# Low halves of split weights formed by an adding transfer, with five vector-engine priorities and a regrouped up-projection

## The chip, the core and the metric

The kernel runs on one core of one Trainium2 chip. The metric is the device time of one execution in microseconds (us). The core has a tensor engine (PE, with weight loads listed apart as PEld), a vector engine (DVE), a scalar engine (ACT), GpSimd (POOL), the sync engine (SP), which here only issues transfers, and 16 DMA engines, which all queues share. Each engine runs its own instructions in a fixed order and waits at the head of that order for semaphores.

## What is computed

A trunk of two layers over 1024 tokens of width 1024. Each layer normalises its input, projects it with one wide matrix, runs four head groups on parts of the projection (A: matrix memory, B: RWKV-7 with a delta rule, C: a gated linear recurrence, D: retention), gates each with its own SiLU path, and maps the four results back with one output projection, which is normalised and added to the input. Cut to what matters here:

```python
for l in range(DEPTH):                        # 2
    h = rms_norm(x, norm_pre[l])
    p = h @ w_in[l]                           # 1024 x 1024 @ 1024 x 7824
    ...
    decay_logit = rwkv_w0[l] + jnp.tanh(w_lo) @ rwkv_w_up[l]
    a_b = jax.nn.sigmoid(rwkv_a0[l] + a_lo @ rwkv_a_up[l])
    ...
    y = jnp.concatenate([y_a, y_b, y_c, y_d], axis=-1) @ w_out[l]   # 2048 -> 1024
    x = x + rms_norm(y, norm_post[l])
```

## The kernel before, in words

Large products are done in the fp32r type, with three products in place of one: every operand is split into a rounded part (hi) and what is left (lo), and hi x hi, hi x lo and lo x hi are added in PSUM. Activations are split once per layer (`hT`). Weights are split as they are loaded, by `load_piece` (line 365): a transfer on SP brings 128 x 512 values into a tile `raw` (2 buffers), ACT rounds them into `hi` (4 buffers), and DVE subtracts `hi` from `raw` into `lo` (4 buffers). A program on one layer loads 186 such tiles, 372 in all: 180 for channel pieces (`wch`), 64 for token pieces (`wa`, `wd`) and 128 for the output projection (`wo`).

A layer has two stages. In the **mixing stage**, pieces of the input projection and the steps of the head groups share PE. A channel piece (`ch_piece_of`, line 412) uses 2 weight tiles, a token piece (`tok_piece_of`, line 452) uses 4, which are all the buffers there are. `Driver` (line 489) writes the order of the program: it keeps a planner's clock (`Clock`, line 147, with guessed durations for every operation), lets a head group take its next step when the planner says that its inputs are ready, and puts six matmuls of a piece wherever no group is ready; a piece is loaded one piece ahead. Every instruction goes through the recording wrapper on line 255, so nearly all rows of the profile carry that line and are told apart by their tiles. After that the tile framework's own list scheduler sets the final order on each engine; code under `tc.high_priority()` is preferred there among instructions that it holds to be ready.

The head groups carry states from chunk to chunk. Group B (`unit_b`, line 773) keeps `bS`: a matmul `psbc<-bS,TQ` (line 1025), then two DVE instructions, one for each head, write the next `bS` (line 1028). Group A (`unit_a`) keeps `aS` (line 1187) and group D (`unit_d`) keeps `dS` (line 1292), each also with two DVE instructions a chunk. `prep` in group B (line 808) starts with the two up-projections: for each of two outputs a matmul with all 128 rows (`luh`) and one with 64 rows (`lul`); their operand `lora` is brought by 32 transfers issued from POOL (line 822), the only transfers there. POOL also computes the power -0.5 of each normalisation (`rsq`, line 362; 128 of them), which DVE waits for.

In the **output stage** (`out_product`, line 1358) two halves of 512 tokens each run over 16 steps. A step has 24 matmuls of 512 columns, and for the step ahead loads two weight tiles and two activations (`ymix`, `zmix`), 256 KB each. While the second half runs, the first half is normalised and stored (`finish`, line 1398), with further transfers and DVE work.

Of the kernel before, what the change touches and what calls it, by code (L numbers as in the profile page):

```python
# [17 lines left out]
F32 = mybir.dt.float32  # L18
F32R = mybir.dt.float32r
AF = mybir.ActivationFunctionType  # L20
ALU = mybir.AluOpType
# [240 lines left out]
def trunk(ctx: ExitStack, tc, x, wch, wa, wd, wg, wo, pv, gb, lup, lrw, npost, cst, dtab, out):  # L262
# [102 lines left out]
    def load_piece(src, n=512):  # L365

        raw = T("raw", (128, 512))
        lo = T("lo", (128, 512), F32R)
        hi = T("hi", (128, 512), F32R)
        DQ.dma_start(raw[:, :n], src)  # L370
        A.copy(hi[:, :n], raw[:, :n])
        V.tensor_tensor(lo[:, :n], raw[:, :n], hi[:, :n].bitcast(F32), ALU.subtract)
        return hi[:, :n], lo[:, :n]
# [399 lines left out]
    def unit_b(l, P, hTs, j, drv):  # L773
# [34 lines left out]
        def prep(qt):  # L808
# [22 lines left out]
            for n, p in enumerate((wps, aps)):  # L831
                hp = slice(64 * n, 64 * n + 64)
                PE.matmul(p[:, 0:QB], lu[0][:, n, :], lo_[:, n, :], start=True, stop=False)
                PE.matmul(p[:, 0:QB], lu[1][hp], lo_[hp, n, :], start=False, stop=True)
# [108 lines left out]
        def mix(qt):  # L943
# [65 lines left out]
            for e in range(2):  # L1009
                p3 = pss[e][:, 0:CP * 128].rearrange("p (c t) -> p c t", c=CP)  # L1010
                V.tensor_tensor(TQ[:, e::2, 0:64], AR[:, :, 2 + e, :], p3[:, :, 0:64], ALU.subtract)
                V.tensor_tensor(TQ[:, e::2, 64:128], id64.unsqueeze(1).to_broadcast((128, CP, 64)), p3[:, :, 64:128], ALU.subtract)
# [8 lines left out]
            for c in range(CB):  # L1021
# [4 lines left out]
                for h in range(2):  # L1026
                    hp = slice(64 * h, 64 * h + 64)
                    V.tensor_scalar(bS[(n + 1) % 2][hp, hp], yc[64:128, hp], wc[64:128, h, c:c + 1], None, ALU.mult)
# [60 lines left out]
    def unit_a(l, P, hTs, j, drv):  # L1089
# [28 lines left out]
        def mix():  # L1118
# [3 lines left out]
            for qt in range(S // QA):  # L1122
# [35 lines left out]
                for h in range(2):  # L1158
                    D = Ds[h]
                    V.scalar_tensor_tensor(D, pss[h][:, 0:QA], 1.0 / 32, D, ALU.mult, ALU.mult)  # L1160
                    pk.append(D)
# [7 lines left out]
                for c in range(NQ):  # L1169
# [12 lines left out]
                    for h in range(2):  # L1182
                        hp = slice(64 * h, 64 * h + 64)
                        if st is None:
                            V.tensor_copy(st2[hp, 65 * h:65 * h + 65], o[hp, 256 + 65 * h:256 + 65 * h + 65])
                            continue
                        V.scalar_tensor_tensor(st2[hp, 65 * h:65 * h + 65], st[hp, 65 * h:65 * h + 65], sc[hp, c:c + 1],
                                               o[hp, 256 + 65 * h:256 + 65 * h + 65], ALU.mult, ALU.add)
# [23 lines left out]
    def unit_d(l, P, hTs, j, drv):  # L1212
# [28 lines left out]
        def mix():  # L1241
# [5 lines left out]
            for qt in range(4):  # L1247
# [29 lines left out]
                for c in range(2):  # L1277
# [9 lines left out]
                    for h in range(2):  # L1287
# [4 lines left out]
                        V.scalar_tensor_tensor(st2[hp, hp], st[hp, hp], G128[2 * j + h], o[hp, so + 64 * h:so + 64 * h + 64], ALU.mult, ALU.add)  # L1292
# [285 lines left out]
```

## Time and profile before

| What | Value |
|---|---|
| Median of 3 runs | 2529.39 us (2527.3 to 2534.37) |
| The profiled execution's own time | 2524.98 us |
| Span of its instructions | 2523.1 us, mean granted TensorE clock 0.992 |
| Instructions | 45012, of them 32064 matmuls and weight loads |
| Bytes by DMA | 265.82 MB, mean 105 GB/s |

PE's busy time is from modelled ends, so that a busy PE may still be a waiting one; its waits are read from the weight loads (PEld), which stand at the head of the same queue. A wait row names the engine and the tile that waits, what it waited for, and the total in us, how often, and the longest.

### The profile page before, as it was taken

Reading aid. Unit: us, or ns where it says so; the run is one execution under the profiler, and the core shown is the slowest. Engines: PE = TensorE matmul, PEld = TensorE weight load, DVE = VectorE, ACT = ScalarE, POOL = GpSimd, SP = SyncE. Lnnn points to the kernel's source line nnn. Section 1 sums busy time; section 2 is a strip of 40 time slices with the busy share of each in tenths; the row PEclk is TensorE's granted clock in tenths of the full one; section 3 lists DMA queues with packets and bytes.
Section 4 is the critical chain, followed back from the end, with each engine's and each line's share of the span. In section 5 each row is a group of like instructions: output and inputs, shape, how many; then the busy total and the mean of one; then the engine's idle time right before and its main releaser. Section 6 shows DMA issues by size and latency. Waiting matters only on the chain.

```text
span 2523.1 us, 45012 instructions
## 1 busy us (share of the span) xinstructions
PE 2383.7 (94%) x16032; PEld 1955.2 (77%) x16032; DVE 1794.0 (71%) x5724; ACT 1054.0 (42%) x2325; POOL 193.7 (8%) x306
## 2 busy tenths in 40 slices
PE   7999999999999999999999999999999999999998
PEld 5797887787787777887677878877877877788876
DVE  6678878878778875435577787888788778744464
ACT  5334433543543553323354344335445435522233
POOL 1201100010000000000012001000000000000000
PEclk9999999999999999999999999999999999999999
DMA  5323233232222233655633232332323222326564
GB/s 160 101 72 88 62 78 99 67 84 71 91 76 75 75 88 103 194 162 176 196 119 103 68 93 74 78 90 68 81 72 90 69 79 76 102 94 217 172 198 153
DMA packets 219237, 265.82 MB, mean 105 GB/s; under 512 B 72708, under 2 KB 122244, under 8 KB 219012
## 3 DMA queue, kind: packets, MB, share of 16 engines
q1 hardware_dynamic: 210308, 254.54, 33.9%
q0 software_dynamic: 8704, 8.39, 1.4%
q8 instruction: 127, 2.08, 0.3%
q14 instruction: 98, 0.80, 0.1%
HBM read 201.76 MB, written 61.08 MB: 104 GB/s over the span
## 4 chain that ended last, share of the span: by engine, by line
PE 47%; DVE 28%; DMA 10%; issue 8%; POOL 4%; ACT 2%; SPq 2%; DVEq 0%; POOLq 0%; ACTq 0%
PE pspj L255 31%; PE psbc L255 9%; PE psmx L255 7%; DVE NT L255 4%; DVE pr L255 4%; DMA PA<-pd 4%; DVE t L255 3%; DVE lo L255 2%; DVE bS L255 2%; POOL sm L255 2%; DVE bt L255 2%; DMA raw<-in_wo_dram 2%; DVE inv L255 2%; SPq L255 2%; DVE sm L255 1%
## 5 line engine op out<-in xcount | busy, mean ns | idle before, releaser
L255 PE MATMUL pspj<-hT,hi 128*128 128x512 f32 x2880 | 940.2, 405 | 2.1 <-DVE hT L255 1.4
L255 PEld LDWEIGHTS pspj<-hT,hi 128*128 128x128 f32 x2880 | 522.0, 190 | 106.7 <-issue 2.5
L255 PE MATMUL pspj<-hT,lo 128*128 128x512 f32 x1440 | 569.8, 396 | 0.0
L255 ACT CAST hi<-raw 128x512 fp32r<-128x512 f32 x372 | 230.0, 619 | 470.0 <-PE pspj L255 266.2
L255 PE MATMUL pspj<-hi,hT 128*128 128x256 f32 x2048 | 409.9, 290 | 0.0
L255 DVE TENSOR_TENSOR lo<-raw,hi 128x512 fp32r<-128x512 f32 x372 | 257.2, 693 | 152.4 <-ACT hi L255 150.9
L255 PEld LDWEIGHTS pspj<-hi,hT 128*128 128x128 f32 x2048 | 331.5, 192 | 6.7 <-issue 1.6
L255 PEld LDWEIGHTS pspj<-hT,lo 128*128 128x128 f32 x1440 | 272.5, 189 | 58.9 <-DVE lo L255 0.2
L255 PE MATMUL pspj<-lo,hT 128*128 128x256 f32 x1024 | 291.1, 284 | 0.1
L255 PEld LDWEIGHTS pspj<-lo,hT 128*128 128x128 f32 x1024 | 197.0, 192 | 0.8 <-DVE lo L255 0.5
L255 POOL TENSOR_TENSOR sm<-sm,mhalf 128x4 f32<-128x4 f32 (+1 forms) x96 | 90.8, 946 | 1227.1 <-DVE sm L255 1141.4
L255 DVE SCALAR_TENSOR_TENSOR NT<-PA,NT 128x23 f32<-128x23 f32 (+13 forms) x768 | 142.9, 235 | 49.0 <-DMA PA<-pd 45.4
L255 PE MATMUL psbc<-hi,pr 128*128 128x512 f32 x384 | 130.7, 394 | 0.0
L255 PE MATMUL pspj<-hi,pr 128*128 128x512 f32 x384 | 130.7, 394 | 0.0
L255 DVE SCALAR_TENSOR_TENSOR pr<-c,pv,pr 128x512 f32<-128x512 f32 x144 | 107.3, 745 | 15.8 <-ACT pr L255 14.9
L255 ACT ACTIVATE t<-t 128x256 f32<-128x256 f32 (+1 forms) x132 | 53.9, 411 | 150.7 <-DVE t L255 126.7
L255 PE MATMUL psmx<-pr,t 128*128 128x65 f32 (+3 forms) x768 | 108.3, 276 | 0.2 <-DVE t L255 0.2
L255 PEld LDWEIGHTS psmx<-pr,t 128*128 128x128 f32 x768 | 96.9, 192 | 1.3 <-DVE t L255 0.3
L255 PE MATMUL psmx<-hi,pr 128*128 128x512 f32 x256 | 91.2, 397 | 3.5 <-ACT pr L255 2.0
L255 DVE TENSOR_TENSOR inv<-PA,NT 128x24 f32<-128x24 f32 (+13 forms) x480 | 87.1, 181 | 8.4
L255 DVE TENSOR_TENSOR NT<-NT,inv 128x24 f32<-128x24 f32 (+13 forms) x480 | 86.6, 180 | 7.2
L255 DVE TENSOR_SCALAR bS<-psbc,wc 64x64 f32<-64x64 f32 x256 | 74.2, 290 | 17.2 <-PE psbc L255 9.8
(273 smaller groups left out, 3824.2 us busy)
## 6 DMA issues: line engine op xcount, KB each, us to landing
raw<-in_wch_dram SPq DMA_DIRECT2D x180, 256.0 KB
raw<-in_wo_dram SPq DMA_DIRECT2D x128, 256.0 KB
PA<-pd SPq DMA_DIRECT2D x64, 256.0 KB
zmix<-c SPq DMA_DIRECT2D x64, 256.0 KB
rkv<-ymix SPq DMA_DIRECT2D x64, 256.0 KB
rkv<-c SPq DMA_DIRECT2D x48, 256.0 KB
rkv<-rkv SPq DMA_DIRECT2D x32, 384.0 KB
lora<-lora POOLq DMA_DIRECT2D x32, 256.0 KB, 3.5
```

What stands on the lines that cost most here:

```text
L255: res = fn(*args, **kw)
```

## The change

`load_piece` no longer subtracts on DVE. ACT writes -`hi` into `lo`, and a transfer issued from POOL reads the same weights from HBM a second time and adds them onto `lo`, which gives weights - hi as before. Five groups of DVE instructions are put under `tc.high_priority()`: the subtractions that write `TQ`, the next `bS`, the products with scores in group A, the next `aS` and the next `dS`. In `prep` the two 128-row matmuls of the up-projections now stand side by side, and after them the two 64-row ones. No buffer count is changed. The planner sees the new instructions through the same wrapper.

```diff
@@ -369,7 +369,8 @@
         hi = T("hi", (128, 512), F32R)
         DQ.dma_start(raw[:, :n], src)
         A.copy(hi[:, :n], raw[:, :n])
-        V.tensor_tensor(lo[:, :n], raw[:, :n], hi[:, :n].bitcast(F32), ALU.subtract)
+        A.activation(lo[:, :n], hi[:, :n].bitcast(F32), AF.Copy, scale=-1.0)
+        Pl.dma_start(lo[:, :n], src.bitcast(F32R), accum_op=ALU.add)
         return hi[:, :n], lo[:, :n]
 
     class L:
@@ -829,8 +830,9 @@
             wps = PT("bc")
             aps = PT("bc")
             for n, p in enumerate((wps, aps)):
+                PE.matmul(p[:, 0:QB], lu[0][:, n, :], lo_[:, n, :], start=True, stop=False)
+            for n, p in enumerate((wps, aps)):
                 hp = slice(64 * n, 64 * n + 64)
-                PE.matmul(p[:, 0:QB], lu[0][:, n, :], lo_[:, n, :], start=True, stop=False)
                 PE.matmul(p[:, 0:QB], lu[1][hp], lo_[hp, n, :], start=False, stop=True)
             nps = PT("bc")
             head_sums(nps, kparts)
@@ -1006,7 +1008,8 @@
             for p in range(CP):
                 for h, e in ((0, 0), (1, 1), (1, 0), (0, 1)):
                     PE.matmul(pss[e][64 * h:64 * h + 64, p * 128:(p + 1) * 128], AP[nrow(e), h * CP + p, :], Gt[nrow(e), h, 2 * p + e, 64:192], start=True, stop=True)
-            for e in range(2):
+            with tc.high_priority():
+              for e in range(2):
                 p3 = pss[e][:, 0:CP * 128].rearrange("p (c t) -> p c t", c=CP)
                 V.tensor_tensor(TQ[:, e::2, 0:64], AR[:, :, 2 + e, :], p3[:, :, 0:64], ALU.subtract)
                 V.tensor_tensor(TQ[:, e::2, 64:128], id64.unsqueeze(1).to_broadcast((128, CP, 64)), p3[:, :, 64:128], ALU.subtract)
@@ -1023,9 +1026,10 @@
                 n = qt * CB + c
                 if n:
                     PE.matmul(yc, TQ[:, c, :], bS[n % 2], start=False, stop=True, skip_group_check=True)
-                for h in range(2):
-                    hp = slice(64 * h, 64 * h + 64)
-                    V.tensor_scalar(bS[(n + 1) % 2][hp, hp], yc[64:128, hp], wc[64:128, h, c:c + 1], None, ALU.mult)
+                with tc.high_priority():
+                    for h in range(2):
+                        hp = slice(64 * h, 64 * h + 64)
+                        V.tensor_scalar(bS[(n + 1) % 2][hp, hp], yc[64:128, hp], wc[64:128, h, c:c + 1], None, ALU.mult)
                 if c + 1 < CB:
                     yield STEP
             drv.flush("B")
@@ -1157,7 +1161,8 @@
                         PE.matmul(pss[h][:, sl], k[hp, sl], q[hp, sl], start=True, stop=True)
                 for h in range(2):
                     D = Ds[h]
-                    V.scalar_tensor_tensor(D, pss[h][:, 0:QA], 1.0 / 32, D, ALU.mult, ALU.mult)
+                    with tc.high_priority():
+                        V.scalar_tensor_tensor(D, pss[h][:, 0:QA], 1.0 / 32, D, ALU.mult, ALU.mult)
                     pk.append(D)
                 sc = small(NQ)
                 V.tensor_copy(sc, qsb.rearrange("p (c t) -> p c t", t=128)[:, :, 127])
@@ -1184,8 +1189,9 @@
                         if st is None:
                             V.tensor_copy(st2[hp, 65 * h:65 * h + 65], o[hp, 256 + 65 * h:256 + 65 * h + 65])
                             continue
-                        V.scalar_tensor_tensor(st2[hp, 65 * h:65 * h + 65], st[hp, 65 * h:65 * h + 65], sc[hp, c:c + 1],
-                                               o[hp, 256 + 65 * h:256 + 65 * h + 65], ALU.mult, ALU.add)
+                        with tc.high_priority():
+                            V.scalar_tensor_tensor(st2[hp, 65 * h:65 * h + 65], st[hp, 65 * h:65 * h + 65], sc[hp, c:c + 1],
+                                                   o[hp, 256 + 65 * h:256 + 65 * h + 65], ALU.mult, ALU.add)
                     st = st2
                     yield STEP
 
@@ -1289,7 +1295,8 @@
                         if st is None:
                             V.tensor_copy(st2[hp, hp], o[hp, so + 64 * h:so + 64 * h + 64])
                             continue
-                        V.scalar_tensor_tensor(st2[hp, hp], st[hp, hp], G128[2 * j + h], o[hp, so + 64 * h:so + 64 * h + 64], ALU.mult, ALU.add)
+                        with tc.high_priority():
+                            V.scalar_tensor_tensor(st2[hp, hp], st[hp, hp], G128[2 * j + h], o[hp, so + 64 * h:so + 64 * h + 64], ALU.mult, ALU.add)
                     st = st2
                     yield STEP
                 ep = small(4)
```

The final order moves in these places. First DVE, in group B's walk over chunks in the mixing stage of layer one (`bS` is the state, `NT` and `inv` belong to the triangular inversion of the next block, `t` and `sm` to group A, `lo` is a weight tile). Before:

```order
L255 TENSOR_TENSOR t_1861<-pr_912,t_1861 128x256
L255 TENSOR_SCALAR bS_103<-psbc_1933,wc_964 64x64
L255 TENSOR_TENSOR lo_1580<-raw_1579,hi_1581 128x512
L255 TENSOR_SCALAR bS_103<-psbc_1933,wc_964 64x64
L255 SCALAR_TENSOR_TENSOR NT_1973<-PA_1766,NT_1973 128x19
L255 SCALAR_TENSOR_TENSOR t_1864<-psmx_2047,t_1864 128x256
L255 SCALAR_TENSOR_TENSOR NT_1973<-PA_1766,NT_1973 128x18
```

Now:

```order
L255 TENSOR_TENSOR t_1885<-pr_924,t_1885 128x256
L255 SCALAR_TENSOR_TENSOR NT_1980<-PA_1768,NT_1980 128x19
L255 SCALAR_TENSOR_TENSOR NT_1980<-PA_1768,NT_1980 128x18
L255 TENSOR_SCALAR bS_103<-psbc_1957,wc_976 64x64 x2
L255 SCALAR_TENSOR_TENSOR NT_1980<-PA_1768,NT_1980 128x17
L255 SCALAR_TENSOR_TENSOR t_1888<-psmx_2071,t_1888 128x256
```

The two halves of a state now stand together (x2), and the weight's subtraction is gone. In the whole program 96 of the 128 pairs of `bS` were parted by other rows before, and 4 are now; of the 56 pairs of `aS` 24 were parted and none is now.

Second PE, at the up-projections of one block of group B. Before:

```order
L255 MATMUL psbc_1933<-bS_104,TQ_1918 128x128
L255 MATMUL psbc_2126<-lora_2118,luh_832 128x256
L255 MATMUL psbc_2126<-lora_2118,lul_833 128x256
L255 MATMUL psbc_2127<-lora_2118,luh_832 128x256
L255 MATMUL psbc_2127<-lora_2118,lul_833 128x256
L255 MATMUL pspj_1832<-hi_1232,hT_479 128x256
```

Now:

```order
L255 MATMUL psbc_1957<-bS_104,TQ_1942 128x128
L255 MATMUL psbc_2150<-lora_2142,luh_842 128x256
L255 MATMUL psbc_2151<-lora_2142,luh_842 128x256
L255 MATMUL psbc_2150<-lora_2142,lul_843 128x256
L255 MATMUL psbc_2151<-lora_2142,lul_843 128x256
L255 MATMUL pspj_1856<-hi_1253,hT_485 128x256
```

The two `luh` products and the two `lul` products are now neighbours.

Third POOL, in the mixing stage (`sm` and `smB` are the powers of the normalisations that DVE waits for). Before:

```order
L255 DMA lora_3490<-lora_271 128x2x256
L255 MEMSET bt_2814 128x4
L255 TENSOR_TENSOR smB_2783<-smB_2780,mhalf 128x4
L255 TENSOR_TENSOR sm_2855<-sm_2852,mhalf 128x4
L255 TENSOR_TENSOR sm_3112<-sm_3109,mhalf 128x4
```

Now:

```order
L255 DMA lo_2976<-in_wch_dram 128x512
L255 TENSOR_TENSOR smB_2851<-smB_2848,mhalf 128x4
L255 DMA lo_2983<-in_wch_dram 128x512
L255 TENSOR_TENSOR sm_3025<-sm_3022,mhalf 128x4
L255 DMA lo_3166<-in_wa_dram 128x512
L255 DMA lo_3173<-in_wa_dram 128x512
L255 MEMSET Nt_3777 32x4x32 x2
L255 TENSOR_TENSOR sm_3276<-sm_3273,mhalf 128x4
L255 DMA lo_3180<-in_wa_dram 128x512
```

The weights' transfers now stand between the powers, in one queue that runs in order; POOL issues 404 transfers where it issued 32.

## Rows read from the trace of the kernel before

**Rows 1.** Parts 1 and 4 of the page: busy time by engine; chain that ended last.
```profile
PE 2383.7 (94%) x16032; PEld 1955.2 (77%) x16032; DVE 1794.0 (71%) x5724; ACT 1054.0 (42%) x2325; POOL 193.7 (8%) x306
...
PE 47%; DVE 28%; DMA 10%; issue 8%; POOL 4%; ACT 2%; SPq 2%; DVEq 0%; POOLq 0%; ACTq 0%
```
**Rows 2.** Busy time by engine, granted clock, DMA share, GB/s: one mixing stage, four output stretches.
```profile
130.00:1000.00 870.00, 825.38 (x6386) 685.27 (x6385) 683.78 (x2434) 383.95 (x887) 69.67 (x115) 0.99 0.29 80
...
1080.80:1169.90 89.10, 89.10 (x385) 71.95 (x383) 35.39 (x58) 27.20 (x48) 0.56 (x1) 1.00 0.48 150
1169.90:1249.90 80.00, 75.70 (x313) 57.76 (x313) 50.72 (x93) 30.95 (x64) 4.17 (x7) 1.00 0.69 220
2331.00:2420.00 89.00, 88.74 (x384) 71.61 (x382) 35.91 (x58) 27.77 (x50) 0.56 (x1) 1.00 0.46 149
2420.00:2500.00 80.00, 76.92 (x325) 60.72 (x326) 49.73 (x83) 27.45 (x48) 1.66 (x3) 1.00 0.68 220
```
**Rows 3.** Waits of the weight loads (PEld): what for, total us, times, longest us.
```profile
PEld psbc L255 <- DVE bS L255: 35.0, 61, 1.7
...
PEld psmx L255 <- DVE t L255: 26.4, 28, 2.4
...
PEld psbc L255 <- DVE bl L255: 14.5, 12, 2.3
...
PEld psmx L255 <- DVE dS L255: 10.7, 10, 2.4
...
PEld psbc L255 <- DVE TQ L255: 6.0, 8, 1.6
```
**Rows 4.** PE in order of time, at an up-projection: start us, us, instruction.
```profile
287.94 0.28 PE L255 MATMUL pspj<-lo,hT 128*128 128x256 f32 x1
288.06 0.28 PE L255 MATMUL pspj<-hi,hT 128*128 128x256 f32 x1
...
288.32 0.36 PE L255 MATMUL psbc<-lora,luh 128*128 128x256 f32 x1
288.62 0.38 PE L255 MATMUL psbc<-lora,lul 64*128 64x256 f32 x1
```
**Rows 5.** Groups of instructions, whole program: count, busy us, mean ns, idle before and why.
```profile
L255 DVE TENSOR_TENSOR lo<-raw,hi 128x512 fp32r<-128x512 f32 x372 | 257.2, 693 | 152.4 <-ACT hi L255 150.9
L255 ACT CAST hi<-raw 128x512 fp32r<-128x512 f32 x372 | 230.0, 619 | 470.0 <-PE pspj L255 266.2 <-PE psbc L255 97.0 <-DMA raw<-in_wo_dram 92.8
```
**Rows 6.** DMA queues, part 3 of the page: packets, MB, share of 16 engines.
```profile
q1 hardware_dynamic: 210308, 254.54, 33.9%
q0 software_dynamic: 8704, 8.39, 1.4%
```
**Rows 7.** ACT and PE in order of time, one output step of the first half.
```profile
1091.42 0.62 ACT L255 CAST hi<-raw 128x512 fp32r<-128x512 f32 x1 [3.91 <-PE psbc L255]
...
1091.94 0.62 ACT L255 CAST pr<-rkv 128x512 fp32r<-128x512 f32 x1
...
1092.46 0.62 ACT L255 CAST hi<-raw 128x512 fp32r<-128x512 f32 x1
...
1097.72 0.39 PE L255 MATMUL psmx<-lo,pr 128*128 128x512 f32 x1
```
**Rows 8.** Tile lora: the 32 transfers issued from POOL (ns), and their landing (us).
```profile
L255 POOL DMA_DIRECT2D lora<-lora x32: 713/746/866, 40.2 to 2112.5; - x32
...
DMA to landing us min/median/max: 3.0/3.5/6.3
```
**Rows 9.** Waits, whole program: PEld for lo in the pieces; ACT's casts; DVE for POOL.
```profile
PEld pspj L255 <- DVE lo L255: 0.8, 3, 0.3
...
ACT hi L255 <- PE pspj L255: 266.2, 150, 5.2
...
DVE t L255 <- POOL sm L255: 56.5, 60, 1.4
```
**Rows 10.** Waits from 1169.9 to 1249.9, the stretch with the normalisation in it.
```profile
PEld psmx L255 <- DVE lo L255: 7.2, 12, 1.4
```

## The prediction, made before the changed kernel had run

> **What bounds the kernel now.** I read the page's busy times and its chain first, then busy time by stage, then the waits of PE's weight loads. PE is busy 94% of the span and holds 47% of the chain that ended last; DVE is second in both, with 71% and 28% [rows 1]. By stage there are two kernels. In the mixing stage PE is busy 825 of 870 us and DVE 684, 79%; the DMA engines have a share of 0.29 [rows 2]. In the output stage PE is full (89.1 of 89.1 us) and DVE slack, while the DMA share is 0.48 in the first stretch and 0.69 where the first half is normalised beside the second half's products [rows 2]. So a lighter DVE can help in the mixing stage alone, and more transfers can hurt most in the output stage. What PE loses to DVE is seen in the waits of its weight loads: 35.0 us for `bS`, 26.4 for `t`, 14.5 for `bl`, 10.7 for `dS`, 6.0 for `TQ` [rows 3].
>
> **What the change gives.**
>
> 1. The order of the up-projections. Two neighbouring 256-column products of equal height start 0.12 us apart, but a 64-row one starts 0.30 us after a 128-row one [rows 4]. A block has four products and paid about 0.31 us for each, 1.24 us with the step to what follows; grouped, it is two steps of 0.12 and two of 0.31, 0.86 us. 32 blocks times 0.38 us is 12 us of PE, in a stage where PE is the fullest engine: **-12 us**, nothing at the other bound.
>
> 2. The priorities. `bS`, `dS` and `TQ` make PE wait 51.7 us [rows 3]; that is the upper bound, and nothing the lower. The order shows that 96 of 128 pairs of `bS` were parted by other DVE work, often a 0.69 us subtraction [rows 5], and 4 are now. A wait for `bS` is 35.0 / 61 = 0.57 us, about one such instruction, so most of it should go. I take two thirds: **-34 us**.
>
> 3. DVE without the subtractions. 372 x 0.693 = 257 us of DVE busy time go [rows 5], 169 of them (244 tiles) in the mixing stages, where DVE's share falls from 79% to about 70%. What the priorities don't touch and this can shorten are the waits for `t` and `bl`, 40.9 us [rows 3]: bounds 0 and -41, and I take a third, **-14 us**. In the output stage PE is full, so there it gives at most the waits for `lo` (below).
>
> **What the change costs.**
>
> 4. DMA engines in the output stage. Each weight tile of 0.262 MB is read twice. The first stretch holds 385 / 24 = 16 steps with 32 tiles, 8.4 MB in 89.1 us or 94 GB/s more; at the stretch's 0.48 for 150 GB/s that is a share of 0.30, so 0.78. The second has 13 steps, 85 GB/s more at 0.69 for 220: 0.27, so 0.96 [rows 2]. POOL's queue now costs 0.167% of the span for each MB against 0.133% on the other queue, 1.25 times [rows 6], which makes it 0.86 and 1.03: over full by 0.03 x 80 = 2.4 us, twice. No row shows an adding transfer. Below, it costs no more than that, and `raw`, which ACT now frees 0.7 us earlier than DVE did, lands sooner: PE's 7.2 us of waits for `lo` in this stretch [rows 10] could go in both layers, -14. Above, it counts as two plain transfers, since source and tile are both read: shares 1.08 and 1.23, so 7 and 18 us, twice, +50. Nearest is the POOL queue's own price, but near a full share queues grow: **+18 us**.
>
> The Trainium skill (Collectives: The Full Stack, section on the bandwidth ceiling and fold count) says that an add in the DMA path runs at half a copy's rate because two sources are read; no run here shows it yet, and by it this term would be the +50 and the sum +17 instead of -15.
>
> 5. The wait for the transfer in a steady output step. ACT starts one cast every 0.52 us. After `hi` at 1091.42 and `pr` at 1091.94, -`hi` would run from 1092.46 to 1093.1, the second `hi` follows, and its negative ends at 1094.1. PE first uses the first `lo` at 1097.72 and the second three products (0.7 us) later [rows 7]. A POOL transfer of this size lands 3.5 us after its issue (3.0 to 6.3) [rows 8]: 1096.6 and 1097.6, so 1.1 and 0.8 us in hand. **Nothing**, covered by the one-step lead; with a landing of 6.3 us each step would be 1.7 to 2.0 us late.
>
> The Trainium skill (SBUF — State Buffer, section on its two separate sides) warns that transfers issued from POOL starve while DVE runs its two-port modes. The trace disagrees: 32 issues took 713 to 866 ns beside a DVE that is 79% busy [rows 8, 2]; by that rule the landing would be near the 6.3 end.
>
> 6. Token pieces. Their last two tiles can be loaded only as the piece ahead lets go of its buffers. `lo` then needs 0.62 + 3.5 us instead of 0.69, 3.4 us more; 16 pieces give 55 us at most. Now such waits come to 0.8 us [rows 9], and the new order puts other products ahead of the last tiles: **+8 us**.
>
> 7. POOL's queue. A `hi` cast stands 266.2 / 150 = 1.8 us at ACT's head until PE frees its buffer [rows 9]; its -`hi` and its transfer stand behind it, and behind that transfer a power that DVE waits for (56.5 us now [rows 9]). If one power in three meets that, 128 / 3 x 1.8 = 77 us of DVE waiting; at DVE's 28% of the chain [rows 1] 21 us. Bounds 0 and 21, half: **+10 us**.
>
> 8. ACT gets 372 x 0.619 = 230 us [rows 5], 42% to 51% busy; at its 2% of the chain **+5 us**. The mixing stage's own transfers, 10% of the chain [rows 1], meet more traffic: **+4 us**, less than 2% of them.
>
> The sum is -60 + 45 = -15 us. On the profiled execution's 2524.98 us that is 2510; that execution lay 4.4 us under the median of the runs shown, so for a median I say **2514 us**, 0.6% faster.
>
> **The rivals.**
>
> - The DMA engines become the bound of the output stage (slower). Mechanism: an add must read both the weights and the tile, so that it counts as two transfers, in the 64 steps of `out_product`. For it: the second stretch has only 0.31 of share left [rows 2]. Against it: POOL's queue alone costs 1.25 times, not 2 [rows 6]. It decides once an added tile costs more than some 1.15 plain ones in the second stretch and 1.7 in the first. Price +50 in place of +18, 2546; if landings also near 6.3 us, another 1 us in about 30 steps, 2576. At three transfers it would be some +150 instead. The Trainium skill's page on collectives, named in step 4, has this rule.
> - POOL's ordered queue gives the DVE gain back (no change): the powers wait, DVE stands in the middle of its normalisations, and step 3 becomes 0 while step 7 costs 21: -60 + 14 + 45 + 11 = +10, but if the token pieces cost nothing, +2. About 2531. For it: the order has a transfer ahead of nearly every power. Against: most tiles have a whole piece of lead.
> - The states were the real limit (much faster): all 51.7 and 41 us of waits go and the output stage costs +5: -105 + 32 = -73, 2456.
> - The priorities don't act: the scheduler weighs them only among what it holds to be ready, and the rows that DVE is late on at run time are others. Then -26 + 45 = +19, 2548. The joined pairs in the order speak against it.
>
> **How the numbers follow.** A measurement of this kernel can tell about 0.3%, 7.6 us, from no change. The forecast has 0.40, its own range 2480 to 2521; the much faster case 0.08; no change 0.13; the DMA bound 0.34; priorities without effect 0.05. So faster is 0.48, the same 0.13, slower 0.39. The range runs from the much faster case to the DMA bound with late landings and some worse adds, 2460 to 2600; three transfers for an add and half of the much faster case lie outside, some 0.15.
>
> **What would show it.** Right: PE's waits for `bS` under 15 us, DVE near 1540 us busy, up-projections 0.12 us apart within a pair, output stretches as long as before at a DMA share under 1. Wrong: output steps well over 5.6 us with PE waiting for a transfer into `lo`; a landing far above 3.5 us; DVE waiting for POOL for 100 us and more; the mixing stages no shorter.

## The result, and the profile after

The changed kernel takes **2718.36 us** (median of 4 runs, 2708.93 to 2730.59) against 2528.35 us for the kernel before on the same chips: ratio 1.0753, 95% interval 1.071 to 1.0797. It is 190 us slower, where the prediction said 2514 us and allowed up to 2600. The profiled execution has a span of 2707.1 us (2523.1 before).

The first place to look is the split by stage. An output stretch is counted here from the first product of `hi` or `lo` with `pr` into the banks `psmx` to the last one of that layer; the rest is mixing. All in us, read from the start times of those products in each trace:

| run | mixing 1 | output 1 | mixing 2 | output 2 | tail |
|---|---|---|---|---|---|
| before | 1080.8 | 178.3 | 1071.5 | 174.5 | 18.0 |
| the change | 1121.5 | 231.0 | 1103.4 | 233.0 | 18.1 |
| difference | +40.7 | +52.7 | +31.9 | +58.5 | +0.1 |

So 111 us were lost in the two output stages, which are a seventh of the time, and 73 us in the mixing, which was to become shorter. The page of the change, parts 1, 3 and 4 (busy time, DMA queues, chain that ended last):

```profile
PE 2439.5 (90%) x16032; PEld 1988.5 (73%) x16032; DVE 1579.5 (58%) x5352; ACT 1256.8 (46%) x2697; POOL 518.2 (19%) x678
...
q1 hardware_dynamic: 210308, 254.54, 31.8%
q0 software_dynamic: 62272, 105.93, 23.2%
...
PE pspj L255 12%; DMA lo<-in_wo_dram 4%; PE psmx L255 3%; PE psbc L255 3%; DVE NT L255 1%; DMA PA<-pd 1%; DVE pr L255 1%; DVE t L255 1%; DVE bt L255 1%; DMA Nt<-nd 1%; POOL sm L255 1%; DMA lo<-in_wa_dram 0%; DVE inv L255 0%; DMA nd<-NT 0%; POOL lo L255 0%
```

DVE fell by 214 us, a little less than the 257 of its subtractions. Against [rows 6], POOL's queue now carries 97.5 MB more in 23.2% instead of 1.4% of the 16 engines' span. That is 0.232 x 16 x 2707.1 - 0.014 x 16 x 2523.1 = 9484 us of engine time, 97.3 us for each MB; the other queue needs 0.318 x 16 x 2707.1 / 254.54 = 54.1. An added MB costs **1.8 times** a plain one. In the chain a new link stands second: the transfer into `lo`, 4%. This chain could be followed back only to 1659 us and covers 38% of the span, so its shares don't compare with those of [rows 1]; the 4% are 116 us, all at the second output stretch of 233.

Busy time by engine, granted clock, DMA share and GB/s in the change: the mixing stage of [rows 2], and each output stage in two pieces, without and with the normalisation of the first half:

```profile
130.00:1000.00 870.00, 802.97 (x6196) 673.61 (x6196) 632.44 (x2333) 423.15 (x955) 148.18 (x202) 0.97 0.45 104
1121.50:1227.00 105.50, 92.48 (x362) 67.98 (x360) 13.07 (x20) 40.18 (x70) 25.07 (x29) 0.97 0.85 195
1227.00:1334.00 107.00, 84.28 (x319) 62.92 (x319) 39.03 (x73) 49.73 (x98) 28.81 (x36) 0.94 0.90 236
2456.00:2560.00 104.00, 88.37 (x343) 66.29 (x342) 13.06 (x19) 39.39 (x68) 24.35 (x29) 0.95 0.82 190
2560.00:2670.00 110.00, 90.35 (x338) 66.72 (x337) 36.18 (x62) 47.37 (x84) 27.69 (x33) 0.92 0.90 230
```

PE was full in the first and third output piece of [rows 2] at a DMA share of 0.48 and 0.46; now it is busy for 88% and 85% of them at 0.85 and 0.82. The granted clock is 0.92 to 0.97 there, where it was 1.00.

What PE waits for in the change: of the weight loads first (all rows that answer to [rows 3] and to the first row of [rows 9]; `bl` has no row left, PE itself waits 7.9 us for it), then of the matmuls:

```profile
PEld psmx L255 <- DMA lo<-in_wo_dram: 110.6, 85, 4.2
...
PEld psmx L255 <- DVE t L255: 35.5, 33, 3.1
...
PEld psbc L255 <- DVE bS L255: 19.7, 24, 2.4
PEld pspj L255 <- DMA lo<-in_wa_dram: 17.1, 10, 5.2
...
PEld pspj L255 <- DMA lo<-in_wch_dram: 13.5, 5, 4.2
PEld pspj L255 <- DMA lo<-in_wd_dram: 13.5, 10, 2.8
PEld psbc L255 <- DVE TQ L255: 13.3, 6, 3.7
...
PEld psmx L255 <- DVE dS L255: 2.7, 2, 1.4
```

```profile
PE psmx L255 <- DMA lo<-in_wo_dram: 74.4, 70, 3.8
...
PE pspj L255 <- DMA lo<-in_wa_dram: 14.9, 8, 5.0
...
PE pspj L255 <- DMA lo<-in_wch_dram: 11.6, 4, 3.8
PE pspj L255 <- DMA lo<-in_wd_dram: 11.4, 9, 2.6
```

Every weight matrix now has a row of its own; before, the pieces' waits for `lo` were 0.8 us [rows 9]. PE itself stands 74.4 us in the output stages and 37.9 us in the mixing for a transfer into `lo`.

One output step of the change in order of time, ACT, POOL and PE (start, us, instruction, idle before and what ended it), to be read beside [rows 7]:

```profile
1194.17 0.62 ACT L255 CAST hi<-raw 128x512 fp32r<-128x512 f32 x1 [4.21 <-PE psbc L255]
...
1194.83 0.63 ACT L255 ACTIVATE lo<-hi 128x512 fp32r<-128x512 f32 x1
...
1195.75 0.86 POOL L255 DMA_DIRECT2D lo<-in_wo_dram  x1 [4.63 <-ACT lo L255]
...
1196.92 0.86 POOL L255 DMA_DIRECT2D lo<-in_wo_dram  x1 [0.31 <-ACT lo L255]
...
1201.92 0.50 PE L255 MATMUL psmx<-lo,pr 128*128 128x512 f32 x1 [0.54 <-DMA lo<-in_wo_dram]
...
1203.21 0.50 PE L255 MATMUL psmx<-lo,pr 128*128 128x512 f32 x1 [0.33 <-DMA lo<-in_wo_dram]
```

ACT waits 4.21 us for a product to let go of the buffers of `hi`. From there it is 0.62 us to `hi`, 0.63 to its negative, 0.86 for POOL to issue, and the transfer lands when PE has stood 0.54 us for it: 7.75 us from 1194.17 to 1201.92. Two steps' tiles have buffers, so the chain must fit into one step and the few products around it, and a step of 24 products, 5.55 us in [rows 2] (385 in 89.1 us), takes 7.0 us here (362 in 105.5 us). The lead in [rows 7] was 6.3 us, but for a chain of two instructions and no transfer.

DMA issues of the change (tile, count, KB each, median us from issue to landing):

```profile
lo<-in_wch_dram POOLq DMA_DIRECT2D x180, 256.0 KB, 4.5
...
lo<-in_wo_dram POOLq DMA_DIRECT2D x128, 256.0 KB, 6.2
...
lora<-lora POOLq DMA_DIRECT2D x32, 256.0 KB, 3.8
```

The landing that I took from `lora` is still near its 3.5 us [rows 8]; the adding transfers take 4.5 us in the mixing and 6.2 us in the output stage.

### The profile page after: what moved, and what is told of

It reads as the page before. It is cut to its first block, busy times and chain, and to the rows that moved or that the text cites. A ratio compares the mean times of both kernels' runs of the same rounds, so it can differ in the third digit from the quotient of the medians.

```text
span 2707.1 us, 45682 instructions
## 1 busy us (share of the span) xinstructions
PE 2439.5 (90%) x16032; PEld 1988.5 (73%) x16032; DVE 1579.5 (58%) x5352; ACT 1256.8 (46%) x2697; POOL 518.2 (19%) x678
## 3 DMA queue, kind: packets, MB, share of 16 engines
q1 hardware_dynamic: 210308, 254.54, 31.8%
q0 software_dynamic: 62272, 105.93, 23.2%
## 5 line engine op out<-in xcount | busy, mean ns | idle before, releaser
L255 PE MATMUL pspj<-hT,hi 128*128 128x512 f32 x2880 | 953.9, 411 | 1.6 <-ACT hT L255 1.6
L255 PE MATMUL pspj<-hT,lo 128*128 128x512 f32 x1440 | 578.8, 402 | 11.6 <-DMA lo<-in_wch_dram 11.6
L255 POOL DMA_DIRECT2D lo<-in_wch_dram x180 | 157.4, 880 | 814.8 <-ACT lo L255 599.1
L255 ACT ACTIVATE lo<-hi 128x512 fp32r<-128x512 f32 x372 | 233.1, 628 | 6.7 <-PE pspj L255 1.1
L255 DVE SCALAR_TENSOR_TENSOR NT<-PA,NT 128x18 f32<-128x18 f32 (+15 forms) x768 | 144.1, 238 | 102.4 <-DMA PA<-pd 99.0
L255 POOL DMA_DIRECT2D lo<-in_wo_dram x128 | 111.0, 880 | 351.9 <-ACT lo L255 346.5
L255 PE MATMUL pspj<-hi,pr 128*128 128x512 f32 x384 | 143.5, 430 | 0.0
L255 PE MATMUL psmx<-lo,pr 128*128 128x512 f32 x128 | 60.9, 476 | 74.9 <-DMA lo<-in_wo_dram 74.4
L255 DVE SCALAR_TENSOR_TENSOR c<-c,pspj 128x512 f32<-128x512 f32 x64 | 43.9, 685 | 115.9 <-ACT c L255 106.4
L255 PEld LDWEIGHTS psmx<-lo,pr 128*128 128x128 f32 x128 | 24.4, 191 | 112.6 <-DMA lo<-in_wo_dram 110.6
```

The source lines that it names most:

```text
L255: res = fn(*args, **kw)
```

## The experiments

Theories at the start. **T**: the adding transfers alone cost the time, as a path (buffer, ACT, POOL, landing) that is longer than the lead, and as work of the DMA engines. **P**: the priorities reorder the mixing for the worse. Two more came up later: **A**, ACT's longer queue, and **C**, the added traffic that nobody waits for. Ratios are to the kernel before, with 95% intervals. "Base" below is the kernel of the first run. The stretches of all runs, in us, as in the first table:

| run | us | ratio (interval) | mixing 1 | output 1 | mixing 2 | output 2 |
|---|---|---|---|---|---|---|
| e1_prio_order (base) | 2495.68 | 0.9891 (0.9867 to 0.9915) | 1061.8 | 177.5 | 1055.0 | 177.5 |
| e2_add_only | 2720.75 | 1.0788 (1.0755 to 1.0821) | 1120.7 | 243.1 | 1111.9 | 233.8 |
| e3_plain | 2621.87 | 1.0382 (1.0351 to 1.0413) | 1097.2 | 212.0 | 1084.4 | 207.9 |
| e4_wo_dve | 2597.88 | 1.0302 (1.027 to 1.0335) | 1129.4 | 176.6 | 1106.6 | 175.9 |
| e5_act_neg | 2540.66 | 1.0072 (1.0059 to 1.0085) | 1084.5 | 184.1 | 1077.6 | 177.1 |
| e6_no_lo | 2484.24 | 0.9848 (0.9834 to 0.9862) | 1063.1 | 171.6 | 1056.3 | 171.3 |
| e7_depth3 | 2688.03 | 1.0658 (1.0643 to 1.0674) | 1111.6 | 223.4 | 1109.1 | 217.1 |
| e8_order_only | 2508.03 | 0.9944 (0.9924 to 0.9964) | 1071.5 | 178.3 | 1057.3 | 176.0 |
| e9_prio_depth3 | 2495.79 | 0.9867 (0.9847 to 0.9887) | 1068.6 | 174.2 | 1063.8 | 172.7 |
| e10_plain_depth3 | 2598.87 | 1.0278 (1.0251 to 1.0305) | 1092.1 | 201.3 | 1085.6 | 196.1 |
| e11_neg_dve | 2754.22 | 1.0897 (1.0868 to 1.0927) | 1125.3 | 252.6 | 1123.5 | 241.1 |
| e12_act_idle | 2524.38 | 0.9996 (0.9979 to 1.0014) | 1078.0 | 178.2 | 1073.8 | 176.0 |
| e13_spare | 2555.35 | 1.0122 (1.0078 to 1.0166) | 1076.9 | 195.4 | 1074.6 | 188.3 |

One caution holds for all of them: the planner prices every instruction, so an edit can move the whole order that it writes. I count the longest sequence of products, by tile names and shape, that two traces have in the same order, out of PE's 16032. Runs 3, 4, 7 and 10 keep at least 15531 of the change's order, runs 8 and 9 at least 15532 of the base's; these differ by their edit almost alone. Runs 5, 6, 12 and 13 keep only 10582 to 14293 of the base's order, runs 2 and 11 some 12700 and 12600 of the change's, the change 12638 of the base's, the base and run 8 some 14300 and 14400 of the order before. There the new order is a rival for what the mixing gains or loses, and no run tests it by itself.

**1. The change without its transfers.** From the change, in `load_piece`:

```diff
-        A.activation(lo[:, :n], hi[:, :n].bitcast(F32), AF.Copy, scale=-1.0)
-        Pl.dma_start(lo[:, :n], src.bitcast(F32R), accum_op=ALU.add)
+        V.tensor_tensor(lo[:, :n], raw[:, :n], hi[:, :n].bitcast(F32), ALU.subtract)
```

> The priorities and the new order of the up-projections stay, the low parts are made by the vector engine again. Theory T (the adding transfers alone cost the time; they land 4.5 to 6.2 us after their issue where the subtraction took 0.69 us): the rest of the change is worth what the prediction gave it, -12 and -34 us, so about 2482 us, at worst the 2528 us of before. Rival P (the priorities reorder the mixing for the worse, since the two mixing stretches lost 40.7 and 31.9 us and the PE queue's waits for transfers into lo explain only some 25 and 19 us of them): 2545 to 2600 us.

2495.68 us, 26 us under before, all of it in the mixing. P falls: priorities and order gain. They gain 26 us, not the 46 of T. Weight loads' waits in this run:

```profile
PEld psbc L255 <- DVE bS L255: 21.4, 31, 2.6
...
PEld psbc L255 <- DVE TQ L255: 5.7, 4, 2.3
PEld psmx L255 <- DVE dS L255: 5.1, 5, 2.3
```

The waits for `bS` are half as many as in [rows 3] (31 for 61), but each is longer, 0.69 us for 0.57; the three sum to 32.2 us, where they were 51.7.

**2. The transfers without the rest.** The edit the other way round, in the kernel before.

> Only the adding transfer, without priorities and without the new order. Leaves nothing out. Theory T: the parts add up, so the 2718 us of the change plus what the other run gains, about 2765 us if that is 46 us. Rival P: at most 2718 us, 2650 to 2700 us.

2720.75 us; its interval overlaps the change's. What the priorities and the order gain in the base, the change does not show for certain (1.0753 against 1.0788). The weight loads' waits for the states in this run:

```profile
PEld psbc L255 <- DVE bS L255: 51.7, 58, 2.9
...
PEld psbc L255 <- DVE TQ L255: 15.9, 11, 3.0
```

With 4.3 us for `dS` that is 71.9 us, and 35.7 in the change. So the waits are half as long with the priorities, and the time hardly shows it; why is not shown. T's sum of parts fails here, and P's reading too.

**3. The same transfer without the add.** In the change:

```diff
-        Pl.dma_start(lo[:, :n], src.bitcast(F32R), accum_op=ALU.add)
+        Pl.dma_start(lo[:, :n], src.bitcast(F32R))
```

> The whole change, but the transfer into lo overwrites where it added, so lo holds the whole weight and not its low part (a changed computation); bytes, queue, issues and waits are the same. Theory T1 (the adding itself is what is slow: a 2,048 B packet that adds takes 178 ns, one of the hardware queue 84 ns): packets near 85 to 120 ns, landing near 3.5 to 4.5 us, output steps near 5.7 to 6.0 us, time 2540 to 2600 us. Rival T2 (the path is slow whatever the packets do: 0.63 us more on ScalarE, 0.88 us on POOL, a landing of some us, and four lo buffers): output steps stay near 6.9 us and the time stays over 2670 us.

2621.87 us, between the two. DMA queues, landing, and PE's waits of this run:

```profile
q0 software_dynamic: 62272, 105.93, 15.3%
```

```profile
lo<-in_wo_dram POOLq DMA_DIRECT2D x128, 256.0 KB, 4.7
```

```profile
PE psmx L255 <- DMA lo<-in_wo_dram: 50.3, 51, 3.6
```

By the working above this is 0.153 x 16 x 2619.9 - 565 = 5849 us of engine time, 60.0 for each MB: only 1.1 times the other queue. In the trace a packet of 2,048 B takes 178 ns (median) when it adds, 99 ns when POOL's queue copies, 84 ns on the other queue. So of the 222 us between the base and the change some 96 are the add itself, in the same order of the program. The other 126 are the path and the traffic of a second read, whatever it does on arrival, and in the mixing also the other order. The time lies in neither theory's range; both T1 and T2 hold a part.

**4. The output product without the transfers.** The subtraction for the 128 tiles of `wo`, the transfer for the other 244:

```diff
-            w = [load_piece(wo[l, UORD[i], :, 512 * c:512 * c + 512]) for c in range(2)]
+            w = [load_piece(wo[l, UORD[i], :, 512 * c:512 * c + 512], add=False) for c in range(2)]
```

> The whole change, but the 128 tiles of the output product get their low parts from the vector engine as before; the 244 tiles of the mixing keep the adding transfer. Leaves nothing out. Theory T: the output stretches return to 178 and 174 us from 230 and 232, so 111 us come back: 2607 us (2595 to 2620), the mixing stretches still 1122 and 1104 us. Rival P says the same of the output stretches; if the mixing stretches gain as well (because the output stage left the clock low or the queues full), under 2590 us.

2597.88 us; the output stretches are back at 176.6 and 175.9 us. So the 128 tiles of the output product cost 4.5% (1.0753 - 1.0302, some 114 us), and the 244 of the mixing 4.1% against the base (some 104 us, the mixing's other order included).

**5. ACT's part with no transfer.** ACT makes -`hi`, and DVE adds `raw`:

```diff
-        Pl.dma_start(lo[:, :n], src.bitcast(F32R), accum_op=ALU.add)
+        V.tensor_tensor(lo[:, :n], raw[:, :n], lo[:, :n].bitcast(F32), ALU.add)
```

> Priorities and new order; the low parts by ScalarE's - hi and then an addition of raw on the vector engine, no second transfer. The price of ScalarE's 372 activations (628 ns each, 233 us busy) by itself, beside the 2496 us of the run without them. Theory T (the cost of the path is the transfer and its issue on POOL): 2496 to 2512 us, output stretches of 177 us. Rival A (ScalarE's queue is late with it, and the mixing's other work on ScalarE behind it): 2530 to 2560 us, that is 34 to 64 of the 65 us that the mixing lost with a plain transfer.

2540.66 us, 45 us over the base, all in the mixing but 6 us: A's numbers. But DVE also waits for ACT's second instruction here, which run 12 leaves out, and the order of the mixing is another one.

**6. No low part.** In the base, without the subtraction:

```diff
-        return hi[:, :n], lo[:, :n]
+        return hi[:, :n], hi[:, :n]
```

> Priorities and new order; no low part is made at all, the matmuls read hi in its place (the low part of the weights is left out of the computation; the matmuls are as many). What the vector engine's relief alone could be worth. The prediction's third term says 14 us (0 to 41): 2482 us (2455 to 2496). Rival: the vector engine is late for other reasons and the relief is worth nothing: 2490 to 2500 us.

2484.24 us: the relief of DVE is worth 11 or 12 us if the low parts cost nothing. The mixing does not move (1063.1 and 1056.3 us for 1061.8 and 1055.0); the gain is the waits for `lo` in the output stage. By this run that is about all that taking the subtractions off DVE could give here. Of all runs this one has the order furthest from the base's, so the mixing may hide a gain and a loss in it.

**7. Room for a third step.** In the change, `hi` and `lo` of every third output step in four buffers that are idle there:

```diff
+            w = [load_piece(wo[l, UORD[i], :, 512 * c:512 * c + 512], tags=("c", "c") if i % 3 == 2 else ("hi", "lo")) for c in range(2)]
```

> The whole change, but every third step of the output product keeps its two hi and two lo tiles in the four buffers of the tag c, which that stage does not use, so that three steps' tiles can be under way instead of two. Leaves nothing out. Theory L (the transfer into lo starts too late, since a lo buffer comes free only when the step but one before it is done, and lands 6.2 us after its issue): the output stretches fall from 230 and 232 us to the DMA engines' own work, 0.856 x 230.5 = 197 us, 195 to 208 us each: 2640 to 2670 us. Rival B (the DMA engines already bound the stage): landing grows with the depth, the stretches stay over 222 us, 2700 to 2720 us.

2688.03 us; the stretches fell by 7.6 and 15.9 us, between the theories. The window of the first output stretch, then the longest waits of ACT and PE in it:

```profile
1112.00:1335.00 223.00, 188.49 (x731) 144.27 (x731) 52.59 (x93) 98.53 (x181) 59.19 (x71) 0.93 0.90 221
```

```profile
ACT hi L255 <- DMA raw<-in_wo_dram: 70.4, 29, 8.2
...
ACT c L255 <- DMA raw<-in_wo_dram: 29.8, 14, 3.6
...
PE psmx L255 <- DMA lo<-in_wo_dram: 28.1, 18, 3.3
```

With the room, ACT's wait for buffers turns into one for `raw` (`c` is the third step's tile). In the change's first output stretch it stood so:

```profile
ACT hi L255 <- PE psbc L255: 108.2, 28, 7.6
ACT hi L255 <- DMA raw<-in_wo_dram: 9.4, 11, 1.2
```

The DMA share stays at 0.90.

**8. The order alone.** The change's up-projections in the kernel before.

> Only the new order of the up-projections, everything else as before. Leaves nothing out. The prediction's first term: -12 us, a ratio of 0.995 to before, and the priorities then hold the other 14 of the 26 us that both were worth together. Rival: the pairs only move the wait, ratio 1.000, and the priorities are worth all 26 us.

0.9944, 14 us under before, as the prediction's first term had it. By the start times, a block's four up-projections and the step to what follows take 1.23 us before and 0.72 us here (medians), which is 16 us for 32 blocks. The priorities hold the other 12.

**9. The base with the room.** The edits of 1 and 7 together.

> Priorities and new order, low parts by the vector engine, and every third step of the output product keeps its hi and lo tiles in the four buffers of the tag c. Leaves nothing out. Without low parts the output stretches took 171.6 and 171.3 us and with them 177.5 and 177.5 us, the mixing the same: what the vector engine's relief is worth lies in the output stage. Theory W (the lo tiles come a little late there, because their buffers come free late): the third step's room gives those 12 us, 2484 us, ratio 0.985. Rival: the vector engine itself is busy there (the finish of the first half's tiles), no change: 2496 us, ratio 0.989.

2495.79 us, ratio 0.9867: the intervals of this and the base overlap. The output stretches gain 3 and 5 us, the mixing of this trace is longer. No better than the base for certain.

**10. The plain transfer with the room.**

> The run with the plain transfer (lo holds the whole weight), and room for three steps' tiles in the output product. The DMA engines' own work is then 0.76 x 211 = 160 us for an output stretch, under the 177 us of TensorE's. Theory: in the plain run the output stage was late only by the path (ScalarE, POOL's issue, landing) against two steps' room, so with a third the stretches fall from 212.0 and 207.9 to 176 to 184 us, 2555 to 2570 us in all; and what the adding run with the same room kept (223.4 and 217.1 us) is then the adding's work on the DMA engines. Rival: the stretches stay over 200 us, some other wait holds them, and nothing follows for the adding run.

201.3 and 196.1 us, the rival's side: the engines' share is 0.79 in the first and the stage still isn't TensorE's. Waits in the first output stretch:

```profile
ACT hi L255 <- DMA raw<-in_wo_dram: 57.3, 28, 6.5
...
PE psmx L255 <- DMA lo<-in_wo_dram: 13.1, 10, 2.7
```

The third step's tiles add 25.7 us to the first wait and 6.8 to the second. The first reading of the weights, with its two `raw` buffers, is now late as well. So what kept the adding run of 7 long can't be put down to the add's work on the engines alone.

**11. -`hi` on DVE.** In the change:

```diff
-        A.activation(lo[:, :n], hi[:, :n].bitcast(F32), AF.Copy, scale=-1.0)
+        V.tensor_scalar(lo[:, :n], hi[:, :n].bitcast(F32), -1.0, None, ALU.mult)
```

> The whole change, but - hi is made by the vector engine and not by ScalarE. Leaves nothing out. Theory A (ScalarE's queue, not the vector engine, is what the mixing has no room on; its 372 activations cost 45 us in the run that adds on the vector engine): 45 us less than the change, near 2673 us, the gain in the mixing stretches. Rival D (in that run it was the vector engine's second wait that cost the 45 us, and ScalarE's work is free as the prediction had it, +5 us): 2710 to 2735 us.

2754.22 us, 36 us over the change; neither theory had that. The instruction is shorter on DVE, and still the transfer starts later, on average 2.3 us after the cast of `hi` has ended, where it was 1.5 in the change:

```profile
L255 DVE TENSOR_SCALAR lo<-hi 128x512 fp32r<-128x512 f32 x372 | 158.0, 427 | 209.9 <-ACT hi L255 208.8
```

DVE stands 208.8 us for `hi` with its other work queued behind. A short instruction between an engine and a transfer costs by the queue that it stands in; how much of the 36 us is that, and how much the other order, is not told apart.

**12. ACT's load with no reader.** In the base:

```diff
+        for w_ in (256, 48):
+            A.activation(idle[:, 0:w_], hi[:, 0:w_].bitcast(F32), AF.Copy, scale=-1.0)
```

> Priorities and new order, low parts by the vector engine, and behind each hi two small activations on ScalarE (256 and 48 elements of hi, into a tile that nobody reads), about as long together as the 628 ns of - hi. Leaves nothing out. ScalarE's load alone, without a later lo. Theory A (the load on ScalarE's queue is what cost the run that adds on the vector engine 45 us): 2530 to 2550 us, the mixing stretches near 1084 and 1078 us. Rival D (it was the lo tile that came 0.63 us later and the vector engine that waited for it): 2494 to 2508 us, the mixing stretches near 1062 and 1055 us.

```profile
L255 ACT ACTIVATE idle<-hi 128x256 bf16<-128x256 f32 x744 | 243.5, 327 | 13.0
```

That is 243.5 us of ACT, 29 us of time, in the mixing alone (16.2 and 18.8 us). Nearer to A: some two thirds of the 45 us of run 5 come with ACT's load, on an engine that is busy 42% of the span and holds 2% of the chain [rows 1]. Whether the load itself costs them, or the order that the planner writes for it, the run does not tell.

**13. Traffic that nobody waits for.** In the base:

```diff
+        Pl.dma_start(dram.tile([128, 512], F32, tag="spare", bufs=16, name=f"spare_{uid[0]}"), hi[:, :n].bitcast(F32))
```

> Priorities and new order, low parts by the vector engine, and for each of the 372 tiles one more transfer of 256 KB on POOL's queue, from hi to a spare place in memory that nobody reads. Leaves nothing out. The load of the transfers on the DMA engines and of their issue on POOL, without anyone waiting for them. Theory C (the added traffic makes the mixing's own transfers, PA<-pd and rkv<-ymix, late): 2515 to 2545 us, the mixing stretches 10 to 20 us longer each. Rival (only who waits for a transfer pays for it): 2490 to 2505 us, the output stretches under 182 us.

2555.35 us, ratio 1.0122: about 60 us over the base, above C's range; the rival falls. 15.1 and 19.6 us are in the mixing, 17.9 and 10.8 in the output stages. ACT's longest waits for a transfer in this run:

```profile
ACT hi L255 <- DMA raw<-in_wo_dram: 179.0, 91, 4.9
```

It is 90.6 us in the base. The 97.5 MB delay the first reading of the weights, and in the mixing `PA<-pd`, for which DVE waits 68.9 us instead of 39.1 in the base. This also holds POOL's 372 issues and the mixing's other order, which the run does not tell apart from the traffic. The spare copies go from `hi` to memory; the change's second reading goes the other way.

**Where the loss went.** From the base to the change the stretches grow by 108 us (mixing) and 109 us (output).

- Output: run 4 shows that all of it comes from the 128 transfers there. Run 13 prices the traffic at 29 us. PE's waits for `lo`, 74.4 us by the trace, are near the remaining 80. An add costs more engine time than the spare copies of run 13, so this parting is rough, and it leaves out the clock (below).
- Mixing: ACT's load 35 us by its stretches (run 12), traffic and issues 35 us (run 13), PE's waits for `lo` 37.9 us by the trace, together 108. That it fits so well proves little: the same sum for run 3 (35 + 35 + 24.6 of waits) gives 95, and 65 us were measured. The three overlap, the first two hold the order of their runs, and the clock is left out here too. Their shares are not shown. For `PA<-pd` alone DVE waits 99.0 us in the change, more than in run 13.
- PE's own time: for the same 16032 products PE is busy 2352.0 us in the base and 2439.5 in the change: 87 of the 217 us, which PE's waits leave out. The windows of the first mixing stretch and the first output stretch in the base, then of the same two and the second output stretch in the change:

```profile
0.00:1061.80 1061.80, 994.39 (x7248) 828.24 (x7249) 801.12 (x2722) 462.70 (x1045) 94.54 (x152) 0.99 0.33 95
...
1062.00:1239.30 177.30, 172.95 (x731) 136.02 (x731) 89.82 (x155) 61.62 (x117) 4.88 (x8) 1.00 0.56 183
```

```profile
0.00:1121.50 1121.50, 1024.19 (x7249) 849.28 (x7250) 732.37 (x2597) 531.48 (x1170) 202.54 (x277) 0.97 0.49 119
1121.50:1352.50 231.00, 192.36 (x742) 142.40 (x741) 52.80 (x94) 96.13 (x178) 57.88 (x69) 0.96 0.87 212
...
2455.90:2688.90 233.00, 194.75 (x743) 144.50 (x742) 49.24 (x81) 92.30 (x162) 55.87 (x65) 0.94 0.84 203
```

The granted clock is lower in each stage: 0.97 for 0.99 in the mixing, 0.96 and 0.94 for 1.00 and 0.99 in the output, 0.967 for 0.991 over the span. From the last two means, 0.033 x 2707.1 - 0.009 x 2489.9, I estimate its part at 67 us at most, since this also counts the lower clock while PE stood. Runs 12 and 13, where no product waits for a transfer into `lo`, keep 0.99; run 3, with shorter waits, has 0.976. The lower clock goes with PE's standing here, and no run changes it alone.

## Why the prediction was wrong

- **Step 5 failed, and it decided.** It priced the wait for the transfer in a steady output step at nothing, "covered by the one-step lead", with a landing of 3.5 us taken from `lora` [rows 8]. Those transfers ran in the mixing at a DMA share near 0.29; the `wo` tiles land after 6.2 us at 0.85. The step's own other end was near: "with a landing of 6.3 us each step would be 1.7 to 2.0 us late", and 64 steps of that are 109 to 128 us; the two stages lost 111, and run 4 gives all of it back. So close a match is partly luck: PE's waits for `lo` there are 74.4 us, 1.2 us a step, and fall on 43 of the 64 steps. The rest is PE busy for longer, in part at the lower clock, which no term had. DVE's two-port modes, for which step 5 weighed a landing near 6.3 us, can hardly be behind it: DVE is busy 13.07 of 105.5 us in that piece. The error was to price a landing from a quiet stage in a stage that this change itself fills, and to count that end as a rival's extra 1 us in about 30 steps.
- **Step 4 was mis-sized.** It took 1.25 times for an add and counted only what the engines were over full. Measured are 1.8 times for each MB. As an estimate from the shares of the two output stretches (0.87 of 231.0 us, 0.84 of 233.0) the engines' own work there is 201 and 196 us, 44 us over the stretches of before: near this step's upper bound of +50, not its +18. The loss of 111 us is not split further between this and step 5.
- **The rule on adds** that step 4 weighed (the Trainium skill, Collectives: The Full Stack, section on the bandwidth ceiling and fold count: an add in the DMA path at half a copy's rate) is nearly borne out here: 178 against 99 ns for a packet of the same queue. That is the rate alone; no run shows the reason. The 1.25 from [rows 6] was not an add's price at all.
- **Step 8 failed in size**: ACT +5 measured +29 (run 12), and the mixing's own transfers +4 are 35 us with POOL's issues (run 13), both with the order that the planner wrote for them. Multiplying by an engine's share of the chain gave far too little: 2% of the chain says what the engine costs now, not what it costs with 230 us more in its queue, or what the planner makes of them.
- **Step 6**, token pieces, +8 up to 55: PE's waits for `wa` and `wd` are 26.3 us, inside its bounds but three times its value. The 11.6 us for `wch`, the channel pieces, had no term.
- **Step 7**, POOL's queue, +10, showed no such sign: DVE's wait for `sm` is 56.3 us, where it was 56.5 [rows 9]. The row of the change:

```profile
DVE t L255 <- POOL sm L255: 56.3, 57, 1.8
```

- **Step 1 was right**: -12, measured -14 (run 8). Its pairs start otherwise than it said, 0.20 us apart with 128 rows and 0.003 with 64 (medians), where it said 0.12. **Step 3 was right in size by luck, wrong in place**: -14, measured -12 (run 6), but in the output stage and not for `t` and `bl` in the mixing. In that run's order the mixing, where DVE is busy 79% of the time, was not short of DVE time.
- **Step 2 was mis-sized**: -34, measured -12 in the base (runs 1 and 8). The joined pairs in the order are there and half of the waits went; those left are longer. In the change the waits are half of run 2's, and the gain can't be told from nothing.
- **The rival nearest to what came** is the DMA bound. Its place was right; its mechanism, the costly add, holds 96 of the 222 us (run 3), and the other 126 come without any add. Its price, 2546 or 2576 us, was too small, since it counted the engines over full and late landings in half of the steps only; the step as a whole went from 5.55 to 7.0 us, and the mixing paid too.

The signs named beforehand read clearly: output steps over 5.6 us, PE waiting for a transfer into `lo`, a landing far above 3.5 us and a mixing no shorter are all there; DVE waiting over 100 us for POOL is not. Of the signs of being right, the waits for `bS` are 19.7 us where under 15 was asked, and DVE is busy 1579.5 us for 1540.

The best version is the base, priorities and new order with the subtraction on DVE: 2496 us, 1.1% under before and 8% under the change.

## What to carry to other kernels

Before moving 0.7 us of work from an engine to a transfer, write down the whole new path (buffer free, cast, negate, issue, landing) and set it against the lead that the buffers give in the busiest stage, with the landing of a stage as full as the change makes it. Then ask what the work could give if it were free: one run without it (12 us here) is cheaper than any way of hiding it. An engine's small share of the chain is no licence to load it, when other engines wait for what is queued behind. And where a planner writes the order, compare the orders before you read a run as one cause alone.

## What was not expected of the hardware

- A packet of 2,048 B that adds takes 178 ns (median), one that copies on the same queue 99 ns; issuing it takes POOL 880 ns for an add and 554 ns for a copy (means of the `wch` transfers).
- 243.5 us of ACT work that nobody reads came with 29 us more time, on an engine that is idle more than half of the time; the planner's order moved with it.
- Two 64-row products start in the same moment if they stand together: in the change a block's four up-projections start at 310.04, 310.16, 310.37 and 310.37 us, the last two 3 ns apart (3 or 4 ns in all 32 blocks), where a 64-row one stood 0.30 us behind a 128-row one [rows 4].
- The granted clock fell to 0.92 to 0.97 where PE stood for transfers, from 1.00: a mean of its two levels, 2.4 and 1.2 GHz. A product of `lo` in the `psmx` banks took 389 ns at its shortest and 796 ns at its longest.
